# A decoder trunk in split float32: in the re-interleaved seven-product blocks, the sum with B21 is ordered behind the split of B21

## The chip, the core and the metric

The kernel runs on one core of one Trainium2 chip. The metric is device time in microseconds (us) for one execution. A core has engines that each work through a queue of their own: TensorE (PE, matrix products), VectorE (DVE, elementwise), ScalarE (ACT, elementwise and activations), GpSimd (POOL, here mainly an issuer of DMAs that add onto a tile) and SyncE (SP, which issues the weight loads). They wait for each other through semaphores. Weights come from HBM into on-chip buffers by DMA.

## The reference

Two layers of a hybrid decoder trunk on 256 tokens of width 2048, all in float32:

```python
for l in range(DEPTH):                       # DEPTH = 2
    h = rms_norm(x, norm1_g[l])
    z = h @ w_in[l]
    out_a = chunked_sgu(gelu(z[..., :2048]), ...)          # gated spatial unit
    out_b = swa_sink_attention(z[..., 2048:], ...)         # windowed attention with sinks
    x = x + concat(rms_norm(out_a), rms_norm(out_b)) @ w_out[l]
    h2 = rms_norm(x, norm2_g[l])
    x = x + (silu(h2 @ w_gate[l]) * (h2 @ w_up[l])) @ w_down[l]   # inner width 5632
```

The last line holds most of the weights: three matrices of 2048 x 5632 in each layer, read once.

## The kernel before

**Split products.** Every product keeps float32 accuracy with matmuls on a rounded type. A weight tile of 128 x 1024 arrives in a buffer `raw` (8 of them). ACT copies it to the rounded type (`wh`, line 127, 5 buffers), DVE subtracts that from the original (`wl`, line 128, 4 buffers). That pair of steps is the split. PE then runs three matmuls for each half tile (function `mm3`): activation-high with `wh` (line 163), activation-high with `wl` (line 164), activation-low with `wh` (line 165), 128 x 512 each. A standard unit feeds two token halves, so it has 12 matmuls for one split; in the text it is a long unit.

**Seven products.** For ten of the eleven column blocks of the gate and up projections, a 2 x 2 block product with seven multiplications in place of eight is used (class `Lean`). Source block B11 is a gate tile, B12 an up tile of the same rows, B21 and B22 the tiles of the other rows. The weights are recombined on the chip: the tile of B11 gets B12 added to it by a DMA that POOL issues (function `onto`, line 456), then t2 = (B11 + B12) + B22 is formed by DVE, then B22 gets B12 added by another such DMA, and finally t2 gets B21 added by DVE. Each of the seven products takes four tiles (i = 0 to 3); each tile makes a half unit with one split and 6 matmuls. The methods `one` to `seven` each issue one half unit with the loads and sums that go with it. Method `five` forms t2, `six` multiplies with t2, `two` loads B21, multiplies with it and adds it onto t2, `four` multiplies with the result. All elementwise sums of the class go through its method `add`, so they share line 453 in the profile: `t<-raw` is the sum of `five`, `t<-t,raw` the sum of `two`, and `c<-...` are sums of product banks.

**Order of recording.** The table `LEAN` gives each method and tile a step number within 28 steps: `one` 0, 4, 8, 12; `two` 24, 26, 27, 29; `three` 6, 10, 14, 18; `four` 30, 31, 33, 37; `five` 7, 11, 15, 19; `six` 16, 20, 22, 23; `seven` 13, 17, 21, 25. Block n starts at step 28 n, so `four` of one block runs among the first steps of the next. Between half units, standard units (the last gate-up block and the down projection) are dealt in, about 0.28 for each step. This part of the program is the two long stretches of the trace, 290 to 880 us (layer 1) and 1270 to 1870 us (layer 2).

**Order of issue.** What an engine's queue holds is not simply what was recorded. A scheduler in the framework walks the recorded instructions and may put one ahead of others of its engine when it expects its operands early. `tc.issue_after(ins)` restricts it: what is recorded inside the block, on the engine of `ins`, has to stand behind `ins` in that engine's queue. No semaphore is added. `last_wl[0]` is the `wl` subtraction of the split recorded last. In `five`, the sum that forms t2 already stands behind such a block; in `two`, the sum does not.

Of the kernel before, what the change touches and what calls it, by code (L numbers as in the profile page):

```python
# [94 lines left out]
def trunk(ctx, tc, x, xt, w_in, w_q, w_out, w_oa, w_uh, w_gate, w_up, w_down, sgu_w, sgu_g, consts,  # L95
# [16 lines left out]
    def raw_load(src, parts=1):  # L112
        raw = wp.tile([P, 2, NB], F32, tag="raw", name="raw", bufs=8)
        n = 2 // parts
        for i in range(parts):
            nc.sync.dma_start(raw[:, i * n : (i + 1) * n, :], src[:, i * n : (i + 1) * n, :])
        return raw

    last_wl = [None]
# [299 lines left out]
    class Lean:  # L419
# [62 lines left out]
        def two(self, i):  # L482
            b21 = raw_load(self.src(1, 0, i))
            self.half(2, b21, i)
            self.add(self.t2[i], self.t2[i], b21)
            z, bank = self.z, self.bank
            if i == 0:
                for v in ("m0", "c12", "c21", "c22"):
                    z[v] = zp.tile([P, NB], F32, tag="z", name=v)
                nc.scalar.copy(z["m0"], bank[3])  # L490
            elif i == 1:
                self.add(z["c21"], bank[2], z["m0"])
            elif i == 2:
                nc.scalar.copy(bank[2], z["c21"])
                self.add(z["c12"], bank[1], z["m0"])
            else:
                self.add(z["c22"], bank[1], z["c21"])
                self.add(z["c12"], bank[4], z["c12"])
# [908 lines left out]
```

## Time and profile before

| | |
|---|---|
| median of 3 runs | 1925.14 us (1925.0 to 1928.06) |
| the profiled execution, its own time | 1928.26 us |
| its span in the profile | 1926.5 us |
| granted TensorE clock, mean | 0.999 |
| PE busy | 1900.0 us of the span |
| DVE busy | 1684.4 us |
| ACT busy | 1399.8 us |
| POOL busy | 217.8 us |

A group row of the profile reads: line, engine, operation, written tile <- read tiles, shapes, count, then the busy time of the group, the mean ns of one, and the idle time of the engine ahead of these instructions with what ended it. A row of waits reads: engine, tile and line that waited, what it waited for, then total us, how many times, and the longest. A row of the timeline reads: start, length, engine, line, operation, tiles, shapes, count, and in brackets the idle time ahead of it. Buffer numbers are left out of the names. Matmul records overlap: one of 0.39 us starts every 0.23 us, so the idle time of PE in the rows is shorter than what a late operand costs.

### The profile page before, as it was taken

To read this page: it belongs to the slowest core of one execution; us is meant where nothing else is said; L and a number is where in the kernel's file an instruction comes from. 1 tells how busy PE (TensorE), PEld (TensorE's weight loads), DVE (VectorE), ACT (ScalarE), POOL (GpSimd) and SP (SyncE) were. 2 spreads that over 40 slices of the span, in tenths; PEclk is the share of its full clock that TensorE was granted. 3 is DMA by queue.
4 is the path that set the end of the run, shared out by engine and by line. 5 is a ranking of instruction groups with operands and counts; after the bars stand their busy time and mean duration, and the time that the engine had idled before them with its cause. 6 is when DMAs were issued, how large, how long until landed. Compare 5 with 4: busy or idle time off the path is not lost.

```text
span 1926.5 us, 25414 instructions
## 1 busy us (share of the span) xinstructions
PE 1900.0 (99%) x8624; PEld 1545.9 (80%) x8624; DVE 1684.4 (87%) x1834; ACT 1399.8 (73%) x1880; POOL 217.8 (11%) x224
## 2 busy tenths in 40 slices
PE   9999999999999999999999999999999999999999
PEld 7887788888888778787888778888888887787887
DVE  7988988999989889988898888989999888898993
ACT  8668776777767667767776886767777676676774
POOL 0231001110111001100002200011101111011100
PEclk9999999999999999999999999999999999999999
DMA  9973669988988789878568648699888888798873
GB/s 353 261 283 125 193 207 242 240 229 241 256 224 228 232 230 240 242 227 251 182 215 291 193 155 235 206 261 234 236 231 260 229 242 218 228 244 237 230 233 116
DMA packets 123394, 442.15 MB, mean 230 GB/s; under 512 B 13696, under 2 KB 14080, under 8 KB 123264
## 3 DMA queue, kind: packets, MB, share of 16 engines
q1 hardware_dynamic: 94320, 336.59, 49.3%
q0 software_dynamic: 28224, 102.77, 29.5%
q8 instruction: 67, 1.10, 0.2%
q10 hardware_dynamic: 720, 1.18, 0.2%
q14 instruction: 63, 0.52, 0.1%
HBM read 438.39 MB, written 2.10 MB: 229 GB/s over the span
## 4 chain that ended last, share of the span: by engine, by line
PE 87%; DVE 5%; issue 3%; ACT 2%; DMA 2%; POOL 0%; SPq 0%; DVEq 0%; ACTq 0%; POOLq 0%
PE m L164 13%; PE m L163 13%; PE m L165 13%; PE dacc L164 10%; PE dacc L163 10%; PE dacc L165 10%; PE acc L164 3%; PE acc L163 3%; PE acc L165 3%; DVE wl L128 2%; DMA raw<-in_w_up_dram 2%; PE l L163 1%; PE l L164 1%; PE l L165 1%; PE ps_f L246 1%
## 5 line engine op out<-in xcount | busy, mean ns | idle before, releaser
L127 ACT CAST wh<-raw 128x1024 fp32r<-128x1024 f32 (+1 forms) x794 | 822.4, 1050 | 346.4 <-PE dacc L165 168.2
L128 DVE TENSOR_TENSOR wl<-raw,wh 128x1024 fp32r<-128x1024 f32 (+1 forms) x794 | 949.6, 1218 | 114.1 <-ACT wh L127 43.3
L164 PE MATMUL m<-wl,ext 128*128 128x512 f32 x704 | 275.5, 391 | 3.9 <-DVE wl L128 3.7
L163 PE MATMUL m<-wh,ext 128*128 128x512 f32 x704 | 275.9, 392 | 0.0
L165 PE MATMUL m<-wh,ext 128*128 128x512 f32 x704 | 274.6, 390 | 0.0
L456 POOL DMA_DIRECT2D raw<-in_w_up_dram x160 | 138.6, 869 | 1074.4 <-DVE wl L128 395.5
L164 PE MATMUL dacc<-wl,aT 128*128 128x512 f32 x624 | 244.3, 391 | 3.4 <-DVE wl L128 3.3
L163 PE MATMUL dacc<-wh,aT 128*128 128x512 f32 x624 | 245.0, 393 | 0.9 <-ACT dacc L1210 0.8
L165 PE MATMUL dacc<-wh,aT 128*128 128x512 f32 x624 | 243.3, 390 | 0.0
L128 DVE TENSOR_TENSOR wl<-t,wh 128x1024 fp32r<-128x1024 f32 x176 | 212.3, 1219 | 7.4 <-ACT wh L127 4.2
L127 ACT CAST wh<-t 128x1024 fp32r<-128x1024 f32 x176 | 184.6, 1052 | 40.1 <-PE m L165 24.9
L164 PE MATMUL m<-wl,hT 128*128 128x512 f32 x528 | 206.0, 390 | 1.0 <-DVE wl L128 0.8
L163 PE MATMUL m<-wh,hT 128*128 128x512 f32 x528 | 206.8, 392 | 0.0
L165 PE MATMUL m<-wh,hT 128*128 128x512 f32 x528 | 205.7, 390 | 0.0
L164 PEld LDWEIGHTS m<-wl,ext 128*128 128x128 f32 x704 | 132.2, 188 | 35.5 <-DVE wl L128 8.7
L165 PEld LDWEIGHTS m<-wh,ext 128*128 128x128 f32 x704 | 132.2, 188 | 27.2
L163 PEld LDWEIGHTS m<-wh,ext 128*128 128x128 f32 x704 | 132.2, 188 | 27.1
L453 DVE TENSOR_TENSOR t<-t,raw 128x1024 f32<-128x1024 f32 x80 | 97.4, 1221 | 53.6 <-DMA raw<-in_w_gate_dram 53.2
L164 PEld LDWEIGHTS dacc<-wl,aT 128*128 128x128 f32 x624 | 117.3, 188 | 29.9 <-DVE wl L128 6.4
L163 PEld LDWEIGHTS dacc<-wh,aT 128*128 128x128 f32 x624 | 117.2, 188 | 26.5 <-ACT dacc L1210 2.5
L165 PEld LDWEIGHTS dacc<-wh,aT 128*128 128x128 f32 x624 | 117.2, 188 | 24.3
L164 PEld LDWEIGHTS m<-wl,hT 128*128 128x128 f32 x528 | 99.2, 188 | 22.3 <-DVE wl L128 2.3
(218 smaller groups left out, 2829.2 us busy)
## 6 DMA issues: line engine op xcount, KB each, us to landing
raw<-in_w_gate_dram SPq DMA_DIRECT2D x176, 512.0 KB, 5.5
raw<-in_w_down_dram SPq DMA_DIRECT2D x176, 512.0 KB, 5.5
raw<-in_w_up_dram POOLq DMA_DIRECT2D x160, 512.0 KB, 8.3
raw<-in_w_up_dram SPq DMA_DIRECT2D x96, 512.0 KB, 5.2
raw<-in_w_in_dram SPq DMA_DIRECT2D x68, 512.0 KB, 6.6
raw<-in_w_out_dram SPq DMA_DIRECT2D x48, 512.0 KB, 4.3
raw<-in_w_q_dram SPq DMA_DIRECT2D x32, 512.0 KB, 6.2
raw<-in_w_oa_dram SPq DMA_DIRECT2D x16, 512.0 KB, 4.0
```

The lines of the kernel that those rows point to most:

```text
L127: nc.scalar.copy(wh[:, j : j + step, :], src)
L128: last_wl[0] = nc.vector.tensor_tensor(wl[:, j : j + step, :], src, f(wh[:, j : j + step, :]), ALU.subtract)
L163: nc.tensor.matmul(acc, ah, wh, start=first, stop=False, skip_group_check=again)
L164: nc.tensor.matmul(acc, ah, wl, start=False, stop=False, skip_group_check=again)
L165: nc.tensor.matmul(acc, al, wh, start=False, stop=last, skip_group_check=again)
L246: nc.tensor.transpose(ps[:, j, t * P : (t + 1) * P], blocks[t][:, j * P : (j + 1) * P], ident)
L453: nc.vector.tensor_tensor(out, x, y, ALU.add)
L456: anchor[0] = nc.gpsimd.dma_start(dst, self.src(0, 1, i), accum_op=ALU.add)
```

## The change

In `two`, the sum of t2 with B21 is recorded inside an ordering block, so that on DVE it stands behind the `wl` subtraction of B21's own split. Nothing is added, removed or resized.

```diff
         def two(self, i):
             b21 = raw_load(self.src(1, 0, i))
             self.half(2, b21, i)
-            self.add(self.t2[i], self.t2[i], b21)
+            with tc.issue_after(last_wl[0].ins):
+                self.add(self.t2[i], self.t2[i], b21)
             z, bank = self.z, self.bank
```

One line is added, so lines after 484 have a number one higher in the changed kernel. The queues of SP and POOL hold the same instructions in the same order as before. On DVE, 80 sums move (ten blocks, four tiles, two layers). The place shown is one block of layer 1, whose t2 tiles are t_5516, t_5616, t_5691 and t_5756; `raw` is any weight buffer, and c_5855 to c_5857 are its sums of product banks.

DVE before, from the last half units of product six to the sums of the block:

```order
L453 TENSOR_TENSOR t_5516<-t_5516,raw 128x1024
L128 TENSOR_TENSOR wl<-raw,wh 128x1024 x2
L453 TENSOR_TENSOR t_5756<-raw 128x1024
L128 TENSOR_TENSOR wl<-t_5616,wh 128x1024
L128 TENSOR_TENSOR wl<-raw,wh 128x1024
L453 TENSOR_TENSOR t_5616<-t_5616,raw 128x1024
L128 TENSOR_TENSOR wl<-raw,wh 128x1024
L128 TENSOR_TENSOR wl<-t_5691,wh 128x1024
L128 TENSOR_TENSOR wl<-t_5756,wh 128x1024
L128 TENSOR_TENSOR wl<-raw,wh 128x1024
L453 TENSOR_TENSOR t_5691<-t_5691,raw 128x1024
L453 TENSOR_TENSOR t_5756<-t_5756,raw 128x1024
```

The row that follows in the queue is six splits of `raw`, the first of them that of the first B21. So the first sum stood eight splits ahead of the split of the tile that it adds.

DVE in the changed kernel, from the split of the first B21 (the second of the first row's two) on:

```order
L128 TENSOR_TENSOR wl<-raw,wh 128x1024 x2
L453 TENSOR_TENSOR t_5516<-t_5516,raw 128x1024
L128 TENSOR_TENSOR wl<-raw,wh 128x1024 x2
L453 TENSOR_TENSOR t_5616<-t_5616,raw 128x1024
L128 TENSOR_TENSOR wl<-raw,wh 128x1024
L453 TENSOR_TENSOR t_5691<-t_5691,raw 128x1024
L128 TENSOR_TENSOR wl<-raw,wh 128x1024
L453 TENSOR_TENSOR c_5856<-m_5636,m_5854 128x512
L453 TENSOR_TENSOR c_5855<-m_5509,m_5854 128x512
L128 TENSOR_TENSOR wl<-raw,wh 128x1024 x2
L453 TENSOR_TENSOR t_5756<-t_5756,raw 128x1024
L453 TENSOR_TENSOR c_5857<-m_5509,c_5856 128x512
```

The next two rows are the sum that makes c_5855 final and the first split of `four` (`wl<-t_5516`). The four sums now stand in the stretch that also holds the four bank sums.

On PE, in the same block, the piece of the difference (dacc_5818 and dacc_5821 are the two accumulators of one long unit):

```order
 L165 MATMUL m_5636<-wh,hT 128x512
 L163 MATMUL dacc_5818<-wh,aT 128x512
+L163 MATMUL dacc_5821<-wh,aT 128x512
 L164 MATMUL dacc_5818<-wl,aT 128x512
 L165 MATMUL dacc_5818<-wh,aT 128x512
-L163 MATMUL dacc_5821<-wh,aT 128x512
 L164 MATMUL dacc_5821<-wl,aT 128x512
```

A matmul that needs only `wh` is taken ahead of one that needs `wl`. The like happens at twelve such places in the two layers, two to four matmuls each; elsewhere the order of PE's matmuls hardly changes.

## The prediction

> **What bounds the kernel now.** I read the page first, then the two long stretches of seven products by themselves, then PE's waits in them, then the timeline at one of these waits.
>
> ```profile
> span 1926.5 us, 25414 instructions
> PE 1900.0 (99%) x8624; PEld 1545.9 (80%) x8624; DVE 1684.4 (87%) x1834; ACT 1399.8 (73%) x1880; POOL 217.8 (11%) x224
> ...
> 290.00:880.00 590.00, 583.97 (x2600) 479.67 (x2600) 528.81 (x497) 425.37 (x489) 66.70 (x78) 1.00 0.86 237
> 1270.00:1870.00 600.00, 592.51 (x2636) 486.30 (x2635) 539.52 (x504) 434.77 (x499) 64.10 (x74) 1.00 0.86 238
> ```
>
> PE is the bound: 26.5 us of the span are not PE's, and of those 6.0 and 7.5 us lie in the stretches that the change touches (590.00 less 583.97, 600.00 less 592.51). The clock is 1.00 in both. So all that a better order can win here is what PE waits, some 13.5 us of shown idle time and a little that the overlap of matmul records hides. DVE is busy for 528.81 of 590, 90%: it keeps up, but with little to spare. PE's waits in the first stretch, and then in the second:
>
> ```profile
> PE ps_f L246 <- DVE aT L1141: 3.1, 3, 1.3
> PE m L164 <- DVE wl L128: 1.8, 3, 1.0
> PE dacc L164 <- DVE wl L128: 0.9, 2, 0.5
> ...
> PE ps_f L246 <- DVE aT L1141: 2.9, 2, 1.5
> PE dacc L164 <- DVE wl L128: 1.7, 3, 0.7
> PE m L164 <- DVE wl L128: 1.7, 3, 0.8
> PE dacc L163 <- ACT dacc L1210: 0.8, 1, 0.8
> ```
>
> Six of the 13.5 us are transposes that wait for one bank (ps_f); 6.1 us in 11 waits are PE waiting for a late `wl` (1.8 + 0.9 + 1.7 + 1.7); 0.8 us is a late copy by ACT. Why is `wl` late? The group row of the sum with B21, and one place on DVE, ACT and PE:
>
> ```profile
> L453 DVE TENSOR_TENSOR t<-t,raw 128x1024 f32<-128x1024 f32 x80 | 97.4, 1221 | 53.6 <-DMA raw<-in_w_gate_dram 53.2
> ...
> 628.40 2.35 DVE L128 TENSOR_TENSOR wl<-raw,wh 128x1024 fp32r<-128x1024 f32 x2
> 634.80 1.23 DVE L453 TENSOR_TENSOR t<-t,raw 128x1024 f32<-128x1024 f32 x1 [4.05 <-DMA raw<-in_w_gate_dram]
> 635.95 2.35 DVE L128 TENSOR_TENSOR wl<-raw,wh 128x1024 fp32r<-128x1024 f32 x2
> ...
> 629.24 1.06 ACT L127 CAST wh<-raw 128x1024 fp32r<-128x1024 f32 x1 [0.53 <-PE dacc L165]
> 630.64 1.05 ACT L127 CAST wh<-raw 128x1024 fp32r<-128x1024 f32 x1 [0.35 <-PE m L165]
> ...
> 635.39 0.39 PE L164 MATMUL dacc<-wl,aT 128*128 128x512 f32 x1
> 635.61 0.39 PE L165 MATMUL dacc<-wh,aT 128*128 128x512 f32 x1
> 635.84 0.39 PE L163 MATMUL m<-wh,ext 128*128 128x512 f32 x1
> 637.22 0.50 PE L164 MATMUL m<-wl,ext 128*128 128x512 f32 x1 [0.99 <-DVE wl L128]
> 637.56 0.40 PE L165 MATMUL m<-wh,ext 128*128 128x512 f32 x1
> 637.80 0.40 PE L163 MATMUL m<-wh,ext 128*128 128x512 f32 x1
> ```
>
> DVE sits at the head of its queue for 4.05 us, waiting for the load of B21 that the sum wants, while two casts that ACT had ended by 631.69 lie behind it, ready to be split. PE has used up its lead by 635.84 and stands. This is the first sum of the block whose order is shown above. In all, 80 such sums hold DVE idle for 53.2 us; most of it is covered by DVE's lead over PE, the rest is in PE's waits.
>
> **What the change moves, and what that removes.** The sum of a tile stands behind its own split. The split needs ACT's cast, and the cast needs the load, so once the split runs the load has landed: the 53.2 us of DMA waits at these sums go, all of them. No instruction is added. Every split that a sum stood ahead of comes earlier by that sum or stays where it was; the time returns behind B21's splits.
>
> What PE gets back: in the rows above, a matmul starts 0.226 us after the last one in step (635.39, 635.61, 635.84). The wait shown as 0.99 us makes the next two steps 1.38 and 0.34 in place of 0.226 each, so 1.27 us are lost: each wait costs 0.28 more than its idle time. Twelve waits (11 on `wl`, 1 on the copy, which is late because POOL's addition for the same block waited for the delayed sum of `five`): 6.1 + 0.8 + 12 x 0.28 = 10.3 us. Two of the twelve are not the sum's doing:
>
> ```profile
> 1635.47 1.05 ACT L127 CAST wh<-raw 128x1024 fp32r<-128x1024 f32 x1 [3.51 <-DMA raw<-in_w_up_dram]
> 1636.55 1.23 DVE L128 TENSOR_TENSOR wl<-raw,wh 128x1024 fp32r<-128x1024 f32 x1 [2.49 <-ACT wh L127]
> 1637.84 0.50 PE L164 MATMUL m<-wl,ext 128*128 128x512 f32 x1 [0.47 <-DVE wl L128]
> ```
>
> There ACT waits for one of POOL's adding loads, DVE for ACT, PE for DVE; this one and the short one behind it stay: 0.47 + 2 x 0.28, about 1.0 us. So **9.3 us** are removed. Bounds: 6.2 (the 3.1 us by which this execution, 1928.26, lies above the median, 1925.14, may be such waits), and 12 (waits under 0.16 us hide in the overlap of the records and are not counted).
>
> **What it costs.** The four sums now share a stretch with the four bank sums. What has to be counted is DVE's lead. From the rows: two splits start 2.35 - 1.22 = 1.13 us apart, and a sum follows a split likewise (634.80 to 635.95). The bank sums:
>
> ```profile
> 1419.44 1.23 DVE L128 TENSOR_TENSOR wl<-raw,wh 128x1024 fp32r<-128x1024 f32 x1 [0.97 <-ACT wh L127]
> 1420.59 1.28 DVE L453 TENSOR_TENSOR c<-m,m 128x512 f32<-128x512 f32 x2
> 1421.78 2.35 DVE L128 TENSOR_TENSOR wl<-raw,wh 128x1024 fp32r<-128x1024 f32 x2
> ```
>
> Two of them take 1421.78 - 1420.59 = 1.19 us, 0.60 each. PE takes 6 x 0.227 = 1.36 us for a half unit and 2.72 for a long one. With four `wl` buffers DVE can end a split when three units are still to run, less about 1.0 us of its own (the split's 1.22 less the matmul that comes ahead of the first `wl`): a full lead is 3 x 1.36 - 1.0 = 3.1 us, or 4.4 with a long unit among the three. From the end of the first B21's split to the end of the first split of `four`, the changed queue has 7 splits, 4 sums and 4 bank sums: 11 x 1.13 + 4 x 0.60 = 14.8 us. PE meanwhile takes six half units and one long one, 10.9 us. The lead falls by 3.9 us: from 4.4 it ends at 0.5, and PE doesn't stall. Without the four sums it would fall by nothing (10.3 against 10.9), which is the present order. So the change is free where a long unit comes just ahead of the first B21, and costs 3.9 - 3.1 + 0.28 = 1.1 us where none does. Over 20 blocks the bounds are 0 and 22 us. In the block shown a long unit does come ahead (dacc, just before); I take two of 20 blocks as short, **2.2 us**.
>
> [...] Whoever takes the mean of 1.22 for the price gets 11 x 1.22 + 4 x 0.68 = 16.1 us, a fall of 5.2, and a stall in every block.
>
> At nothing I put these. B21's buffer is now held until the sum after its split, 1.13 us longer, so a later load of SP's queue starts later: 80 x 1.13 = 90 us if no load were early. The rows against it: ACT waits 37.5 us for loads in all and those are POOL's adding loads, none of SP's; and this first B21 landed at 634.80, and its split stands eight splits later.
>
> ```profile
> ACT wh L127 <- DMA raw<-in_w_up_dram: 37.5, 26, 3.5
> ACT m L494 <- DVE c L453: 10.2, 10, 2.7
> ```
>
> ACT's copy at line 494 waits for a bank sum, which now has three sums ahead of it; but DVE idled 0.97 us just ahead of it in the present order (1419.44), so it comes later by under a us, and ACT's casts are further ahead than that. PE's `wh` matmuls taken ahead need casts two units early; ACT has five buffers.
>
> **The sum.** The execution of 1928.26 loses 9.3 and gets 2.2 back: -7.1, so 1921.2; taken off the median, **1918.0 us** (1925.14 - 7.1), -0.4%.
>
> **The rivals.**
> *The dense stretch starves PE.* If DVE comes to the first B21 with a lead of 3.1 us or less (no long unit ahead, a transposed block's subtraction in between, a cast that came late), each of 20 blocks costs 1.1 us: 22 - 9.3 = +12.7, **1938 us**. It decides from the lead at that place: a stall of 0.47 us in each block, a lead of 3.7, cancels the gain. For it: the scheduler takes `wh` matmuls ahead of `wl` ones just there, so it expects `wl` late there, and 0.5 us left is less than one copy of ACT. Against: removing 53 us of blocked time is what lets DVE be at full lead.
> *The wait only moves.* ACT's cast of B21 now is what meets the late load, and DVE waits behind ACT; PE loses as before: **1925 us**. For: ACT is a queue in order too. Against: the load lands some eight splits ahead of its own.
> *More goes than I count.* The transposes' waits for ps_f shrink as well, since ACT's and DVE's parts of them are late in the blocks that were late before: 6.0 + 5 x 0.28 = 7.4 more, half the dense cost: 1925.14 - 9.3 - 7.4 + 1.1 = **1909.5 us**. Against: no such sum stands just ahead of them.
> That the order would not change is ruled out by the queues above. [...]
>
> **How the numbers follow.** My forecast 0.55, more than counted 0.09, the wait moves 0.18, the dense stretch 0.18. A difference under 0.2%, 3.9 us, can't be told from no change by these runs. The forecast's own range is 1913 (12 removed, nothing paid) to 1923 (6.2 removed, 4 paid); the last 2 us of it and the moved wait are no change, and a fifth of the dense case stays within 0.2%: faster 0.62, same 0.24, slower 0.14. Range 1910 to 1927: it takes in the third rival at its lower end and all of the second, and leaves out most of the dense case.
>
> **What would show it.** In the changed profile the row of `t<-t,raw` should have nearly no idle time ahead of it (53.6 now). PE's waits for `wl` in the stretches should fall from 6.1 us to under 3, and those left should lie behind a sum with B21, not ahead of B21's split. ps_f's 6.0 us should stand. If the waits for `wl` number 15 or more, right where `four` begins, the dense stretch decides; if DVE's waits for ACT and ACT's for `in_w_gate` grow by tens of us, the wait has only moved. The forecast is wrong at its root if PE's busy time in 290 to 880 us no longer leaves gaps and the span still stands.

## The result, and the profile after

The changed kernel takes 1917.5 us (median of 19 runs), the kernel before, run beside it, 1928.06 (19 runs). The ratio is 0.9947, with a 95% interval of 0.9937 to 0.9956: about 10 us, half a per cent, faster. One of the 19 runs of the changed kernel took 3866.0 us; it is left out of the ratio, and nothing on record says why it was slow. The forecast was 1918.0, taken off the earlier median of 1925.14. The profiled execution of the changed kernel has these first lines on its page:

```profile
span 1914.2 us, 25497 instructions
PE 1892.9 (99%) x8624; PEld 1544.8 (81%) x8624; DVE 1685.7 (88%) x1834; ACT 1400.8 (73%) x1880; POOL 218.2 (11%) x224
```

The span fell by 12.3 us, and DVE, ACT and POOL are as busy as before. Three group rows of DVE (the last number and what follows it is the idle time ahead and its cause), of the sum of `two`, that of `five`, and the scale operation of line 1163 (1162 before):

```profile
L453 DVE TENSOR_TENSOR t<-t,raw 128x1024 f32<-128x1024 f32 x80 | 97.3, 1217 | 0.0
L453 DVE TENSOR_TENSOR t<-raw 128x1024 f32<-128x1024 f32 x80 | 97.4, 1218 | 0.0
L1163 DVE SCALAR_TENSOR_TENSOR c<-c,nr,c 128x512 f32<-128x512 f32 x20 | 14.9, 745 | 5.9 <-ACT c L1162 5.9
```

The 53.6 us of idle time ahead of the sums with B21 are gone. The wait in the third row is new: now DVE waits there for ACT. Before, the row was:

```profile
L1162 DVE SCALAR_TENSOR_TENSOR c<-c,nr,c 128x512 f32<-128x512 f32 x20 | 14.9, 745 | 0.0
```

PE's waits on `wl` and ps_f in the whole span, after the change:

```profile
PE ps_f L246 <- DVE aT L1142: 6.8, 6, 1.8
PE m L164 <- DVE wl L128: 3.0, 3, 1.4
```

Before, in the whole span, they were these, with `dacc` on `wl` and the copy of line 1210:

```profile
PE ps_f L246 <- DVE aT L1141: 6.0, 5, 1.5
PE m L164 <- DVE wl L128: 4.5, 8, 1.0
PE dacc L164 <- DVE wl L128: 3.3, 6, 0.7
PE dacc L163 <- ACT dacc L1210: 0.8, 1, 0.8
```

That is 14.6 us in 20 waits; now it is 9.8 us in 9. Two of the three waits on `wl` left are of 1.4 us and stand at a new place. The timeline of the first of them, on DVE, POOL, ACT and then PE:

```profile
798.37 1.21 DVE L128 TENSOR_TENSOR wl<-raw,wh 128x1024 fp32r<-128x1024 f32 x1
798.98 1.76 POOL L456 DMA_DIRECT2D raw<-in_w_up_dram  x2 [3.92 <-DVE t L453]
800.87 1.05 ACT L127 CAST wh<-raw 128x1024 fp32r<-128x1024 f32 x1 [3.51 <-DMA raw<-in_w_up_dram]
801.83 0.68 ACT L1162 ACTIVATE c<-m,ir 128x512 f32<-128x512 f32 x1
802.54 0.75 DVE L1163 SCALAR_TENSOR_TENSOR c<-c,nr,c 128x512 f32<-128x512 f32 x1 [2.96 <-ACT c L1162]
...
804.48 0.50 PE L164 MATMUL m<-wl,ext 128*128 128x512 f32 x1 [1.43 <-DVE wl L128]
```

ACT waits 3.51 us for an adding load, its Silu comes behind that, DVE stands 2.96 us for the Silu at the head of its queue, and PE stands for the split behind it. In the kernel before, that scale operation stood one split further back in this block.

To see losses too short for the list of waits, I counted each start of a matmul that came more than 0.06 us late against the step of 0.227 us. In the two stretches (285 to 930 and 1255 to 1870 us) this gives 26.2 us before and 16.5 after: a late `wl` 13.5 and 4.4 (with the matmul behind it), ACT's copy 1.7 and 0, ps_f 6.8 and 8.0, the rest 4.1 each. With 1.0 us less elsewhere, and 1.7 us for 3.4 us at a granted clock of 0.50 at 167 us in the execution before alone (nothing to do with the change), that is 12.4 of the 12.3 us of the spans.

### The profile page after: what moved, and what is told of

The parts are those of the page before. It is cut to its first block, busy times and chain, and to the rows that moved or that the text cites. A ratio compares the mean times of both kernels' runs of the same rounds, so it can differ in the third digit from the quotient of the medians.

```text
span 1914.2 us, 25497 instructions
## 1 busy us (share of the span) xinstructions
PE 1892.9 (99%) x8624; PEld 1544.8 (81%) x8624; DVE 1685.7 (88%) x1834; ACT 1400.8 (73%) x1880; POOL 218.2 (11%) x224
## 4 chain that ended last, share of the span: by engine, by line
PE 89%; DVE 4%; ACT 2%; DMA 2%; issue 2%; POOL 0%; SPq 0%; DVEq 0%; POOLq 0%; ACTq 0%
PE m L164 14%; PE m L163 14%; PE m L165 14%; PE dacc L163 11%; PE dacc L164 11%; PE dacc L165 11%; PE acc L164 3%; PE acc L165 3%; PE acc L163 3%; DMA raw<-in_w_up_dram 2%; DVE wl L128 1%; PE l L163 1%; PE l L164 1%; PE l L165 1%; PE ps_f L246 1%
## 5 line engine op out<-in xcount | busy, mean ns | idle before, releaser
L165 PEld LDWEIGHTS m<-wh,hT 128*128 128x128 f32 x528 | 99.1, 188 | 20.5
```

The costliest lines, as they stand in the source:

```text
L165: nc.tensor.matmul(acc, al, wh, start=False, stop=last, skip_group_check=again)
```

## The experiments

Each kernel differs from the one named by the lines shown. All ratios are to the kernel before, run beside it (medians 1925.9 to 1926.9 us).

**Is it the late load?** Three kernels: only the first tile's sum held; only the sums of tiles 1 and 2 held; and the order of before, in which B21 is loaded ahead of product six, so that the sum finds it there.

```diff
 hold_first (against the changed kernel)
-            with tc.issue_after(last_wl[0].ins):
+            with tc.issue_after(last_wl[0].ins) if i in (0,) else ExitStack():
 hold_mid: the same with (1, 2)
 early_load (against the kernel before)
         def six(self, i):
+            self.raw[2, i] = raw_load(self.src(1, 0, i))
...
         def two(self, i):
-            b21 = raw_load(self.src(1, 0, i))
+            b21 = self.raw[2, i]
```

> Of the four sums of a block only the first (tile 0) is held behind the split of its B21; the other three are free as before. Theory L (what the change removes is VectorE's wait at the head of its queue for a late load of B21): in the trace of before the 13 longest of the 24 waits, some 37 of 53 us, are at the first sum, so about two thirds of the change's gain of 10 us comes with it alone: 1919 to 1923 us, 12 to 18 us of waits for the load left at this row. Theory O (what counts is that the sums stand behind the splits, so that the splits come earlier): one sum of four moved, a quarter of the gain: about 1925 us.

> Only the second and third sum of a block (tiles 1 and 2) are held behind their splits; the first and the fourth are free. In the trace of before no wait of any length for the load stands at these two. Theory L: no gain, within 2 us of before, 45 us or more of waits for the load left. Theory O: half of the sums moved, half of the gain: 1922 to 1923 us.

> No sum is held; instead the load of B21 is issued with product six of the same tile, 6 to 8 steps earlier than product two. VectorE's queue stands nearly as in the kernel before. Theory L: the load lands some 13 us earlier than it did, the waits at the sum fall from 53 to under 15 us, and 6 to 11 us of the time go: 1916 to 1921 us, though a buffer is held longer. Theory O: VectorE's order is that of before, so the time is that of before, 1928 us.

Measured: hold_first 1912.5 us, ratio 0.9925 (0.9913 to 0.9936); hold_mid 1971.95, 1.0228 (1.0209 to 1.0247); early_load 1909.2, 0.9914 (0.9900 to 0.9928). The group row of the sum with B21 in hold_first:

```profile
L453 DVE TENSOR_TENSOR t<-t,raw 128x1024 f32<-128x1024 f32 x80 | 97.4, 1220 | 14.8 <-DMA raw<-in_w_gate_dram 14.2
```

The same row in hold_mid:

```profile
L453 DVE TENSOR_TENSOR t<-t,raw 128x1024 f32<-128x1024 f32 x80 | 97.6, 1220 | 107.8 <-DMA raw<-in_w_gate_dram 107.7
```

PE's first waits in hold_mid:

```profile
PE dacc L164 <- DVE wl L128: 24.7, 15, 3.6
PE ps_f L246 <- DVE aT L1142: 7.4, 5, 2.1
PE m L164 <- DVE wl L128: 4.1, 12, 0.9
```

And the row in early_load, whose list of PE's waits holds none on `wl` in these products:

```profile
L453 DVE TENSOR_TENSOR t<-t,raw 128x1024 f32<-128x1024 f32 x80 | 96.8, 1218 | 0.5
```

What is left there is the transposes' wait for their bank:

```profile
PE ps_f L246 <- DVE aT L1142: 5.3, 4, 1.9
```

The time goes with DVE's wait for the load, not with the sums' places in the queue: with the wait doubled the kernel is 45 us slower. With the wait gone and the old order kept it is 18 us faster, more than the change itself; in that run PE's and ACT's queues are those of the kernel before, and of DVE's 1834 instructions 16 stand elsewhere. So the late load at the head of DVE's queue is the loss that the change removes. But no time came out as either theory had it. hold_first was expected at 1919 to 1923 us and early_load at 1916 to 1921, and both are faster; hold_first, with one sum held, is faster than the changed kernel with four, by intervals that just do not touch. The first sum had 42.2 of the 53.2 us, more than the 37 that I had counted. hold_mid's time is far from both that were expected, since the waits did not stay as they were but doubled. I had overlooked that the fourth sum, left free, then comes earlier in DVE's queue: two sums fewer stand ahead of it, and in most blocks also one to four splits fewer. By the trace it waits for its load in all 20 blocks, 67.1 us in all, for 11.1 in the kernel before. In the block shown:

```profile
658.17 1.23 DVE L453 TENSOR_TENSOR t<-t,raw 128x1024 f32<-128x1024 f32 x1 [4.01 <-DMA raw<-in_w_gate_dram]
```

**Is DVE's lead nearly used up?** The changed kernel with one more sum of the same size in each block, behind the fourth. Its result is used by nothing.

```diff
+            if i == 3:
+                with tc.issue_after(last_wl[0].ins):
+                    self.add(b21, b21, self.t2[i])
```

> The changed kernel with one more addition on VectorE of the size of the sum, onto B21's buffer, behind the sum of tile 3 of each block: it leaves the result alone and only takes 1.13 us in the dense stretch. Theory D (the lead of VectorE over TensorE is 0.5 us at the end of the dense stretch, as counted): each of 20 blocks stalls TensorE for 0.6 us and 0.28 more: 14 to 20 us on top of the changed kernel, 1932 to 1938 us. Rival: there is more lead than counted, and it costs under 4 us: 1918 to 1922 us.

Measured: 1941.96 us, ratio 1.0080 (1.0064 to 1.0097), some 25 us over the changed kernel, a little more than expected. PE's waits on `wl` are back:

```profile
PE m L164 <- DVE wl L128: 11.8, 10, 4.5
PE ps_f L246 <- DVE aT L1145: 6.9, 5, 2.1
PE dacc L164 <- DVE wl L128: 3.2, 4, 0.8
```

The lead can be read directly: from the end of the first split of product four to the first matmul that uses it. Over the 20 blocks its mean is 1.97 us before, 0.70 in the changed kernel (least 0.15, never a stall), 2.60 with the early load, and 0.35 here, where many blocks stand at 0.05, which means that PE waits. So the held sums spend the lead almost to the end, as worked out, and the extra 1.13 us overdraw it. But the 14 to 20 us that I had expected, a stall in each block, are not what happened. By the starts of PE's matmuls about 10 us are lost around the first split of `four`, in 13 of the 20 blocks. Two waits of 4.1 and 4.5 us stand at 814 and 1775 us, some 20 us behind that place. And at 565, 814 and 1774 us the granted clock is 0.50 for 3.4, 3.4 and 6.8 us (its mean over the execution is 0.996), in which PE was busy for 11.7 us; at half speed that is about 5.8 us more, an estimate. That the time came near what was expected is in part luck.

**What keeps the change from the early load's gain?** Two further kernels, and one that divides the sums. c21_behind is the changed kernel with the scale operation of line 1163 again one split later in the two blocks where DVE now waits for ACT. early_hold has the changed kernel's order on DVE and PE, instruction by instruction, with the early load.

```diff
 c21_behind (against the changed kernel)
-                later(1, lambda: self.out(1, bank[2], z["c21"], z["c22"]))
+                later(1.75, lambda: self.out(1, bank[2], z["c21"], z["c22"]))
 early_hold (against early_load)
-            self.add(self.t2[i], self.t2[i], b21)
+            with tc.issue_after(last_wl[0].ins):
+                self.add(self.t2[i], self.t2[i], b21)
 hold_03: hold_first with (0, 3)
```

> The changed kernel, in which only two instructions of DVE's queue stand elsewhere: in one block of each layer (at 802 and 1752 us in the changed kernel's profile) the scale operation of line 1163 for c21 again stands one split later, as it did before the change. PE's, ACT's, POOL's and SP's orders are those of the changed kernel. Theory W (what the change gave back is this new wait: DVE stands 2.96 us at the head of its queue for ACT's Silu, and PE loses 1.60 + 0.11 and 1.59 + 0.11 us): the two PE waits on wl with 1.4 us go, the time falls by 3.4 us from the changed kernel's 1917.5 to about 1914, ratio to before 0.993. Theory D (the four held sums eat the lead in every block): the wait moves a unit on or is paid elsewhere, the time stays at 1917 to 1918, ratio 0.9947.

> The changed kernel's order of DVE and PE, instruction by instruction, but B21 is loaded ahead of product six, as in the run with the early load. So in neither of the two does a sum wait for its load; they differ in the four sums' places alone (and the two scale operations of line 1163). Theory W: the early load's 1909 plus 3.4 for the two waits at line 1163, 1912.5, ratio 0.993. Theory D (the dense stretch costs besides): the early load's gain is lost down to the changed kernel's: 1916 to 1918, ratio 0.9945. If the place of the load alone made the difference between the changed kernel and the early load, and the held sums cost nothing: 1909, ratio 0.991.

> Only the sums of tiles 0 and 3 are held behind their splits; those of tiles 1 and 2 stand free, and line 1163 stands as before the change. With tile 0 alone held, 14.2 us of waits of DVE at 13 sums were left and PE lost 0.7 us at one of them. Theory W (holding a sum is free, the waits at line 1163 were the price): the rest of the load waits shrinks, and the time is that of tile 0 alone or up to 1 us less: 1911.5 to 1912.5, ratio 0.992. Theory D: two sums in the dense stretch cost more than one, about 2 us over tile 0 alone: 1914.5, ratio 0.9935.

Measured: c21_behind 1917.95 us, ratio 0.9951 (0.9937 to 0.9965); early_hold 1917.6, 0.9955 (0.9940 to 0.9970); hold_03 1910.9, 0.9918 (0.9904 to 0.9932). The group row of line 1163 in c21_behind:

```profile
L1163 DVE SCALAR_TENSOR_TENSOR c<-c,nr,c 128x512 f32<-128x512 f32 x20 | 14.9, 745 | 0.0
```

PE's longest wait there:

```profile
PE ps_f L246 <- DVE aT L1142: 8.6, 7, 1.9
```

DVE's wait for the Silu is gone (5.9 to 0.0), and the time stands: PE waits for ps_f instead, 8.6 us for 6.8. So the new wait at line 1163 was where a lateness showed, not its cause; theory W falls. PE's waits in early_hold:

```profile
PE ps_f L246 <- DVE aT L1143: 8.1, 6, 1.9
...
PE m L164 <- DVE wl L128: 3.0, 2, 1.6
```

No sum waits for a load in early_hold, nor in early_load, and yet they are 8 us apart with intervals that don't touch. So holding all four sums has a price of its own, about 8 us; with two sums held (hold_03) or one, hardly any of it is seen. That price takes in what the scheduler does along with it: the order of PE's matmuls shown above changes when four sums are held, and in hold_first and hold_03 it is that of the kernel before. No run parts the sums' places from PE's order. In these kernels PE's losses lie at the same six places at most, three in each layer: in the changed kernel 1.9 us at 562, 1.6 at 685, 2.3 at 805 to 810, 1.2 at 1511, 1.6 at 1634 and 2.3 at 1754 to 1759. The second of them in the changed kernel, on ACT, PE and DVE:

```profile
676.68 1.05 ACT L127 CAST wh<-raw 128x1024 fp32r<-128x1024 f32 x1 [2.87 <-DMA raw<-in_w_up_dram]
...
678.74 3.88 ACT L127 CAST wh<-raw 128x1024 fp32r<-128x1024 f32 x4
...
680.31 0.27 PE L246 MATMUL ps_f<-ident,m 128*128 128x128 f32 x1
...
683.99 0.58 ACT L1141 CAST aT<-ps_f 128x512 fp32r<-128x512 f32 x1
...
684.60 0.69 DVE L1142 TENSOR_TENSOR aT<-ps_f,aT 128x512 fp32r<-128x512 f32 x1 [0.16 <-ACT aT L1141]
...
685.35 0.33 PE L246 MATMUL ps_f<-ident,m 128*128 128x128 f32 x1 [1.47 <-DVE aT L1142]
```

ACT waits for an adding load, has then four casts in arrears, and takes the first pair of transposes out of ps_f 3.7 us after PE wrote it; the second pair waits.

**Is it the start of the adding loads?** POOL issues them when DVE is done with the tile (DVE ends 718.0 of the 1074.4 us that POOL idles ahead of them in the kernel before), and in the kernels with four held sums they start 0.5 us nearer to PE's use on the mean. early_lag delays 80 of the 160 in the early load's kernel by an operation of POOL that copies a part of t2 to a spare tile that nothing reads; all other queues stay as they were.

```diff
+            late = nc.gpsimd.affine_select(
+                out=lag, in_=self.t2[i][:, 0, :384], pattern=[[1, 384]], compare_op=ALU.is_ge,
+                fill=0.0, base=0, channel_multiplier=0,
+            )
+            with tc.issue_after(late.ins):
                 self.onto(self.raw[3, i], i)
```

> The kernel with the early load (sums where they were before the change), in which POOL reads 384 columns of each t2 into a spare tile, some 0.7 us, between DVE's sum in product five and the adding load that follows it. The orders of PE, DVE, ACT and SP are those of the early load, instruction by instruction; only 80 of POOL's 160 adding loads start later, by about 0.8 us. In the kernels with all four sums held, the adding loads start 0.5 us closer to PE's use of them than in the others (16.56 us ahead on the mean, against 17.0). Theory P (that is how the held sums cost: DVE late, POOL's load late, ACT's cast late, then PE at six places): the four PE waits for ps_f behind product seven grow, from 5.9 us in all by 0.8 each or more, and ACT's waits for in_w_up grow from 36 us: 1909 plus 3 to 7, 1912 to 1916, ratio 0.993 to 0.995. Theory Q (DVE's own queue is late at these places, the loads are early enough): 1909 to 1910, ratio 0.9915.

Measured: 1909.05 us, ratio 0.9913 (0.9900 to 0.9926), the early load's time. The group row of the added operation:

```profile
L473 POOL TENSOR_SCALAR_AFFINE_SELECT lag<-t 128x384 f32<-128x384 f32 x80 | 93.0, 1162 | 493.5 <-DVE t L454 493.5
```

PE's wait for ps_f, and ACT's for the adding loads, in the lists of waits:

```profile
PE ps_f L247 <- DVE aT L1148: 3.2, 3, 1.3
...
ACT wh L127 <- DMA raw<-in_w_up_dram: 42.5, 28, 3.5
```

The operation takes 1.16 us, the loads started 0.6 to 1.2 us nearer to PE's use, and ACT waited more for them (42.5 us for 36.1), but PE waited less. Theory P, as I had put it, falls: a later start alone costs nothing here. What does go with PE's loss, if not in every row, is the time from the landing of a block's third and fourth adding load (product seven's first tile, product five's third) to the first matmul with that tile's `wl`. My count from the trace, means over 20 blocks, in us, with PE's losses of 0.3 us and more at the six places:

```
kernel         third  fourth   loss   ratio
before          6.8    7.6      6.8   1
changed         6.1    6.7     11.0   0.9947
c21_behind      6.0    6.7     10.3   0.9951
early_hold      6.1    6.7     12.4   0.9955
hold_03         6.8    7.5      6.7   0.9918
hold_first      6.9    7.7      4.4   0.9925
early_load      6.9    7.8      5.9   0.9914
early_lag       7.4    8.3      4.0   0.9913
after_seven0    8.3    6.8      7.8   0.9935
early_seven0    9.6    8.2      1.7   0.9906
```

**More time for these two loads.** In the table of steps product seven's first tile goes from 13 to 14, in the changed kernel and in the early load's; and in the changed kernel also product five's third from 15 to 16.5.

```diff
 after_seven0, early_seven0
-    (16, 20, 22, 23), (13, 17, 21, 25),
+    (16, 20, 22, 23), (14, 17, 21, 25),
 after_both, besides
-    (0, 4, 8, 12), (24, 26, 27, 29), (6, 10, 14, 18), (30, 31, 33, 37), (7, 11, 15, 19),
+    (0, 4, 8, 12), (24, 26, 27, 29), (6, 10, 14, 18), (30, 31, 33, 37), (7, 11, 16.5, 19),
```

> The changed kernel, all four sums held, with product seven's first tile recorded one step later (14 in place of 13), so that the adding load on that tile has one more unit, 1.4 to 2.7 us, until ACT's cast of it. Theory P: of the 11 us that PE loses at the six places, 7.9 lie behind that cast (685, 805, 810, 1634, 1754, 1759 us) and most of them go; the 3.1 us at 562 and 1511, behind product five's load, stay: 1917.5 less 5 to 8, 1910 to 1912.5, ratio 0.991 to 0.9925. Theory Q: no gain, 1917, ratio 0.9945; the waits for ps_f stay at 6 to 8 us.

> The early load together with product seven's first tile one step later. Theory P: the 5.9 us that PE still loses behind that cast go too: 1909 less 4 to 6, 1903 to 1905, ratio 0.9885. Theory Q: 1909, ratio 0.991. The early load holds a buffer longer and the later step another, so SP's loads could start late instead: then ACT waits for in_w_gate, and the time is 1910 or above.

> The changed kernel, all four sums held, with product seven's first tile one step later (14 in place of 13) and product five's third tile behind product six's first (16.5 in place of 15). These are the two tiles whose adding loads have the least time between landing and PE's use: 6.1 and 6.7 us on the mean in the changed kernel, 6.9 and 7.5 to 7.8 in the kernels with one or no sum held and no wait. With seven's tile moved alone the first became 8.3 us, the second stayed at 6.8, and PE's loss at the six places fell from 11.0 to 7.8 us. Theory M (the held sums cost through the margin of these two loads): the second becomes about 8 us, the losses at 565 and 1511 us (2.2 + 1.3) go and the others shrink: 1912.9 less 3 to 6, 1907 to 1910, ratio 0.9905 to 0.992. Rival (DVE's own lead is what is short): nothing more goes, 1912 to 1914, ratio 0.9935 or above; a later five also makes its sum and the next adding load later, which by itself would cost.

Measured: after_seven0 1912.9 us, ratio 0.9935 (0.9922 to 0.9948); early_seven0 1907.9, 0.9906 (0.9892 to 0.9920); after_both 1922.5, 0.9977 (0.9966 to 0.9987). Where the third load had more time, PE's loss at the six places fell, from 11.0 to 7.8 us and from 5.9 to 1.7. The ratios went the same way, by about 2 us (0.9947 to 0.9935) and 1.5 us (0.9914 to 0.9906), but the intervals of each pair overlap, so the gain in time is not shown, and both times lie between those of the two theories. after_both is a miss. Its waits:

```profile
PE m L163 <- ACT m L476: 5.9, 2, 3.6
...
PE m L164 <- DVE wl L128: 2.3, 4, 0.8
PE m L163 <- ACT wh L127: 1.7, 2, 1.4
...
ACT wh L127 <- DMA raw<-in_w_up_dram: 55.3, 25, 7.3
```

No wait for ps_f is left (6.9 before this step), as theory M wanted. But the later `five` makes its own sum and the next adding load later: the seventh load's time to its use fell from 8.0 to 5.2 us, and PE lost at other places (332, 812, 1283 and 1765 us) more than it had won. The run says nothing on the fourth load by itself.

**A wider step between the two pairs of transposes**, with the early load:

```diff
-                later(2 + c, ready)
+                later(2 + 2 * c, ready)
```

> The early load, and in every block the second pair of transposes of the gated product is recorded two units after the first in place of one. PE's order changes. Tests what the remaining waits of PE for the bank ps_f are (5.3 us in 4 waits with the early load). If the second pair waits because the first has not left the bank: the waits go, 5.3 + 4 x 0.28 = 6.4 us less, about 1903, ratio 0.988. If the first pair waits (DVE comes late to the operations that empty the bank): no gain, 1909, ratio 0.991. If the later pair delays the down projection's units and these the order of the splits: a loss of several us.

Measured: 1913.8 us, ratio 0.9934 (0.9920 to 0.9948). The waits for ps_f go, and this one comes in their place:

```profile
PE m L164 <- DVE wl L128: 5.3, 3, 2.8
```

At 687, 1636 and 1758 us, where the transposes had waited, the next unit now waits for its `wl`. As with line 1163, the wait only changed its name; my reading, not shown, is that ACT and DVE are late there whatever PE asks for first. The loss against the early load (0.9934 for 0.9914) is not shown, since the intervals overlap.

The fastest kernel of all is early_seven0, 1907.9 us: the load moved ahead, no sum held. Against it early_load and early_lag can't be told apart; the changed kernel is behind it by an interval that does not touch.

## Why the prediction was right, and where its terms were not

That the total came within half a us (1918.0 for 1917.5) is luck. The forecast was taken off a median of 1925.14 from three runs, and beside the changed kernel the kernel before took 1928.06, 2.9 us more; the gain was about 10 us in place of 7.1, 3 us more. The two cancel. The gain itself has the right sign and order of size, from a mechanism that the runs bear out, but by two terms that were both too small.

- **What bounds the kernel.** Right. PE is the bound, and the time follows its waits in every run.
- **The cause.** Right, and shown: the late load at the head of DVE's queue (early_load above all, and hold_mid). All 53.2 us of DVE's waits for it are gone.
- **9.3 us given back to PE.** Too small. In the changed kernel the old waits on `wl` and on the copy are gone everywhere but for one of about 0.2 us: by the same rule (idle time and 0.28 each) 12.8 us less 0.5, 12.3. The term fell short because the prediction's windows ended at 880 us; the last block of layer 1 has its sums after that. The rows of the kernel before from 880 to 950 us:

```profile
PE m L164 <- DVE wl L128: 1.0, 2, 0.6
PE dacc L164 <- DVE wl L128: 0.7, 1, 0.7
```

1.7 us and 3 x 0.28 make 2.5, and the 1.0 us that I had kept back as not the sum's went too, or came back as part of ps_f. The upper bound of 12 was nearer than the value taken. Even this is not all that the late load cost: without it and without held sums the kernel is 18 us faster (early_load).
- **2.2 us for the dense stretch.** This step failed in its place and its size. The lead was rightly worked out: 0.5 us left at the first split of `four`, measured 0.70 on the mean. In the block shown it starts at 4.41 us and ends at 0.15, and DVE took 15.1 us where 14.8 were counted. No block stalls there, not two of 20 as I had taken. The failing step was to stop there. I took a lead that stays above nothing to be free. The runs don't bear that out: holding all four sums costs about 8 us (early_hold against early_load), and PE loses time some 20 us further on, at places where ACT also waits for an adding load. That it is the small lead that costs there is argued, not shown. For it: hold_03, whose mean lead is 1.6 us, does not pay. Against: after_seven0 has the changed kernel's lead, about 0.7 us, and loses less at these places (7.8 us for 11.0). By the rows of the changed kernel it is 3.4 us behind line 1163 (2 x 1.43 and 2 x 0.28) and 1.1 at ps_f, 4.5 against the kernel before, which lost at these places too.
- **At nothing:** the buffer held longer did no harm (no wait of ACT for `in_w_gate`). ACT's copy at line 494 did not come later but waits less, 1.1 us for 10.2. What I had not listed at all is that the scheduler would take the scale operation of line 1163 a split earlier in two blocks; c21_behind shows that this by itself costs nothing that the runs can tell.
- **The rivals.** The moved wait: refuted, there is no such wait at ACT. ACT does take its queue in order where the trace of before lets one see it: it waits 3.51 us ahead of the cast at 1635.47, and the copy of line 1210 behind that cast starts at 1636.42, though the copy that it needs had ended at 1631.96. More than counted: refuted, ps_f grew from 6.0 to 6.8 us. With the first sum alone held it would have come true in part (3.7). The dense stretch: its place was wrong, for no block stalls there; what holding four sums costs kept the gain at 10 us in place of 14 to 18, and its reason (too little lead left) may be part of that.
- **The signs.** The row without idle time came; the waits on `wl` in the stretches fell to 3.0, just the bound named. Those left did not lie behind a sum with B21, and ps_f did not quite stand: these two signs pointed to the term that was wrong, the price of the dense stretch.

What stays open: why with four held sums the third and fourth load land 0.8 us nearer to their use. 0.6 us of it is a later start, but early_lag had as late a start for the third load and not the late landing. In the changed kernel the second load starts 2.4 us nearer to its use than with the early load, and the third may queue behind it; that was not tried. Nor was PE's changed order tried by itself.

## What to carry to other kernels

Here a sum that waited for its load at the head of DVE's queue blocked ready work behind it (4.05 us in the block shown, with two casts ready): moving the load ahead was worth more (18 us) than moving the instruction back (10). The instruction, moved back, takes its engine's time in another place and spends the lead there (0.70 us left on the mean, of 1.97), which is the likely reason. When an order is made denser, don't stop where the lead is still above nothing; follow it to the next place where another wait (here for an adding load) may draw on the same lead. And when removing a wait leaves the time as it was and another one grows, look for what both have ahead of them.

## What the runs showed of the hardware that was not expected

**A short half-clock stretch behind a wait of PE of 2 us.** In hold_03, the wait in PE's timeline:

```profile
807.26 0.33 PE L246 MATMUL ps_f<-ident,m 128*128 128x128 f32 x1 [1.93 <-DVE aT L1142]
```

Two windows behind it (window, busy time of PE, PEld, DVE, ACT and POOL, then granted clock, DMA share, GB/s):

```profile
807.60:811.00 3.40, 3.40 (x11) 2.76 (x10) 2.47 (x3) 0.59 (x1) 0.00 (x0) 0.52 0.94 213
811.00:814.00 3.00, 3.00 (x15) 2.46 (x14) 1.23 (x1) 1.06 (x1) 0.00 (x0) 1.00 1.03 343
```

Such stretches of 3.4 us, by the halved clock about 1.7 us of lost time each (an estimate, half of 3.4), followed waits of that size in the seven products in hold_03 (two), early_load and c21_behind (mean granted clock of the execution 0.998 in each), but not in early_hold or after_seven0 (1.0 and 0.999), whose longest waits there are 1.9 and 2.0 us. At 166 to 168 us every one of the fourteen kernels has a wait of PE of 1.96 to 1.99 us, and in nine of the fourteen traces such a stretch stands at that place: in the kernel before the clock is 0.50 from 167.0 to 170.4 us, in the changed kernel it is 1.00 there. With the stretch behind it the wait in hold_03 thus cost nearly twice what its row says (1.93 us and some 1.7); in early_hold a wait of 1.9 us had none behind it.

**A later adding load took less time.** On the mean over the 20 blocks, the third load took 8.0 us from issue to landing with the early load and 6.9 with the lag, so that it landed no later in relation to PE. The median of all 160 adding loads is 8.1 and 7.7 us. Here the start of such a load did not tell when it ended.
